# Long convolution in the frequency domain: the filters' spectrum K in one copy, four frequencies on each half of the partitions

## The chip, the core and the metric

The kernel runs on one core of a Trainium2 chip. Its engines work side by side, each through a queue of its own in order: PE multiplies matrices (PEld are its weight loads), DVE (VectorE) and POOL (GpSimd) work elementwise, ACT (ScalarE) copies, casts and applies functions, and SP (SyncE) issues the DMAs. The metric is the device time of one execution in microseconds (us).

## The reference

One block of a diffusion backbone of two layers: attention, then a Hyena layer. The change touches only the second, on 1024 tokens x 1024 channels:

```python
def long_conv(u, k_f, skip):
    L = u.shape[1]
    uf = _f32(u)
    y = jnp.fft.irfft(jnp.fft.rfft(uf, n=2 * L, axis=1) * k_f, n=2 * L, axis=1)[:, :L]
    return (y + uf * _f32(skip)).astype(u.dtype)

def hyena_mixer(h, w_in, conv_w, conv_b, ..., freq, skip, w_out):
    p = h @ w_in                                    # four times the width
    u = short_conv(p[..., :(HY_ORDER + 1) * HY_WIDTH], conv_w, conv_b)
    gate = p[..., (HY_ORDER + 1) * HY_WIDTH:]
    parts = jnp.split(u, HY_ORDER + 1, axis=-1)
    k_f = hyena_filters(L, ...)
    z = parts[0]
    for o in range(HY_ORDER):                       # HY_ORDER = 2
        z = parts[o + 1] * long_conv(z, k_f[:, o], skip[o])
    return (z * jax.nn.silu(gate)) @ w_out
```

So for each of two orders and each channel a signal is transformed, multiplied by the filter's spectrum k_f, with the skip weight added to it, and transformed back.

## The kernel before, in words

The filters' spectra are made early, next to the attention, and lie in DRAM as `Kd`. After the attention comes the stage that the change touches, the function `projections`: 32 jobs (four kinds times eight blocks of 128 channels) multiply the normed tokens by `hy_w_in`, each product as three matmuls on high and low parts (`mm3`, L100 to L102), into a PSUM tile `pw`. The weights are split into `wh` (ACT, L1711) and `wl` (POOL, L1712) a job ahead. The stage is cut into pieces of two `mm3`; after each piece the functions run that a table `plan` holds for its number, put there by `at(piece, function)`. That fixes by hand the order of the instructions on PE, ACT, DVE and POOL. The order of SP's DMAs is not written by hand: it is laid down when the program is built, by when each is expected to be ready. Each engine keeps to its order, so one that waits holds up all behind it.

Sixteen convolutions (two orders, eight blocks) run between the projections, one begun every 13 pieces (`start`, `PERIOD`). `conv(o, b)` places its steps s_ pieces after its start:

- 0 to 3, `first`: one stage of the transform on PE, a copy by ACT (L1827, tile `caT`), a store to DRAM (`ad`, L1828).
- 4, `regroup`: `ad` is read back in another order as two tiles `cau` (L1833).
- 11, 13, 15, 17, `spectrum(0)` to `spectrum(3)`: each takes four of sixteen frequency groups through eight matmul passes (L1854) into a PSUM bank `ps` from `pq`, with real parts on partitions 0 to 63 and imaginary ones on 64 to 127. Then DVE multiplies by K: two products across the halves into `cB` (L1857, L1858), one in place into `cA` (L1860), and their sum (L1861).
- 4 pieces behind each, `back`: matmuls (L1871), a copy by ACT into `cbT` (L1873), a store `bd` (L1876).
- 22 and later: `regroup_back` loads `spare` (L1881), `split_back` splits it (ACT `cih` L1887, DVE `cil` L1888), `last` does the last matmuls on `IA`, `end` multiplies into the gated product `u` (L1913).

`pq()` hands out PSUM banks in turn, so a matmul may wait for the engine that still reads its bank. Between these steps DVE does the short convolutions (L1781 to L1784), POOL the low halves `z1l` (L1905) and the gates (L1773).

K comes by `kernel_load(uc)`, four times in a convolution, two of them at piece 4, the others at pieces 12 and 14. Each fills a tile of 128 partitions with two DMAs (L1842) of the same 64 rows, one to each half, since `spectrum` reads K at the partitions of its PSUM operand. For the first there is also the skip row `skp` (L1839), a DMA that overwrites row 64 of the tile, where a real coefficient of its own lies (L1844), and two memsets (L1845, L1846). POOL adds the skip weights (L1847). Two buffers serve K, so a load waits until the `spectrum` two before it has been read by DVE.

Of the kernel before, what the change touches and what calls it, by code (L numbers as in the profile page):

```python
# [9 lines left out]
F32 = mybir.dt.float32  # L10
# [98 lines left out]
def backbone(tc, I, out):  # L109
# [1704 lines left out]
    def conv(o, b):  # L1814
# [20 lines left out]
        def kernel_load(uc):  # L1835
            us = slice(4 * uc, 4 * uc + 4)
            if uc == 0:
                B["skp"] = yp.tile([P, P], F32, tag="skp", bufs=2, name=nm("skp"))
                nc.sync.dma_start(B["skp"], I["hy_skip"][0, o, b * P:(b + 1) * P].partition_broadcast(P))  # L1839
            K = yp.tile([P, 2, 4, P], F32, tag="K", bufs=2, name=nm("K"))  # L1840
            for h in range(2):
                nc.sync.dma_start(K[64 * h:64 * h + 64], Kv[:, :, us, :])  # L1842
            if uc == 0:
                nc.sync.dma_start(K[64:65, 0, 0, :], Kd[o, b, 64:65, 0:P])  # L1844
                nc.gpsimd.memset(K[0:1, 1, 0, :], 0.0)  # L1845
                nc.gpsimd.memset(K[64:65, 1, 0, :], 0.0)  # L1846
            nc.gpsimd.tensor_tensor(K[:, 0], K[:, 0], B["skp"].unsqueeze(1).to_broadcast([P, 4, P]), ALU.add)  # L1847
            Ks[uc] = K

        def spectrum(uc):  # L1850
            K, au = Ks.pop(uc), B["au", uc // 2]
            ps = pq()
            for i in range(4):
                nc.tensor.matmul(ps[:, i * P:(i + 1) * P], FB[:, 4 * uc + i, :], au[:, 4 * (uc % 2) + i, :], start=True, stop=True)  # L1854
            pv = ps.rearrange("p (u c) -> p u c", c=P)
            B_ = yp.tile([P, 4, P], F32, tag="cB", bufs=2, name=nm("cB"))
            nc.vector.scalar_tensor_tensor(B_[0:64], pv[64:128], -1.0, K[64:128, 1], ALU.mult, ALU.mult)  # L1857
            nc.vector.tensor_tensor(B_[64:128], pv[0:64], K[0:64, 1], ALU.mult)  # L1858
            A1 = yp.tile([P, 4, P], F32, tag="cA", bufs=2, name=nm("cA"))
            nc.vector.tensor_tensor(A1, pv, K[:, 0], ALU.mult)  # L1860
            nc.vector.tensor_tensor(A1, A1, B_, ALU.add)  # L1861
            A1s[uc] = A1
# [59 lines left out]
        at(s_ + 4, lambda: kernel_load(0), regroup, lambda: kernel_load(1))  # L1922
        for i in range(4):
            at(s_ + SP + 2 * i, lambda i=i: spectrum(i))
            if i < 2:
                at(s_ + SP + 2 * i + 1, lambda i=i: kernel_load(i + 2))
# [367 lines left out]
```

## Time and profile before

| | |
|---|---|
| time, median of three runs | 1821.87 us (1821.21 to 1828.35) |
| profiled execution, its own time | 1821.09 us |
| its span | 1819.3 us |
| busy share of the span: PE, DVE, POOL, ACT | 95%, 57%, 48%, 43% |
| DMA over the span | 253.28 MB, mean 139 GB/s |

The span runs from the first to the last instruction; the profiled execution's own time contains it and what lies around. A wait is given as engine and line that waited, then what ended it, the total in us, how often, and the longest. In a row of a timeline the number first is the start in us from the span's beginning, then the duration. In grouped rows the busy time is followed by the mean ns of one instruction, and behind the second bar stands the idle time of the engine just before them and what ended it.

### The profile page before, as it was taken

What the parts mean: (1) busy time and instruction counts of PE and PEld (TensorE: products, weight loads), DVE (VectorE), ACT (ScalarE), POOL (GpSimd) and SP (SyncE); (2) the same over time, 40 slices, a digit from 0 to 9 for tenths busy, and PEclk for the clock granted to TensorE, in tenths of its full rate; (3) what the DMA queues carried; (4) which work ended last, traced back from release to release, by engine and by line L of the source; (5) the groups of instructions that cost most, each with busy time, mean ns of one, the idle gap of its engine ahead of it and who ended that gap; (6) DMA issues with size and microseconds to landing.
All of it is one profiled execution on the core that took longest, in us unless ns stands there. A gap on an engine that the chain in (4) does not pass through costs nothing.

```text
span 1819.3 us, 25906 instructions
## 1 busy us (share of the span) xinstructions
PE 1725.1 (95%) x9616; PEld 1346.1 (74%) x9616; DVE 1029.7 (57%) x1495; ACT 774.3 (43%) x1326; POOL 865.6 (48%) x615
## 2 busy tenths in 40 slices
PE   7999999998999999899999999999999999899898
PEld 2667789986766666666666788888888788788686
DVE  5557757446666665466565323456657555645743
ACT  5878711243545544544444333243343333332431
POOL 2457712534379777577776453234333333244400
PEclk9999999999999999999999999999999999999999
DMA  7766688232120010100010227568787778787633
GB/s 256 246 211 216 210 257 276 64 82 74 43 56 24 11 47 21 39 32 22 22 34 21 81 88 184 161 178 221 215 228 223 223 217 219 209 239 212 196 98 110
DMA packets 245709, 253.28 MB, mean 139 GB/s; under 512 B 30591, under 2 KB 195367, under 8 KB 245167
## 3 DMA queue, kind: packets, MB, share of 16 engines
q1 hardware_dynamic: 243408, 249.53, 46.4%
q10 hardware_dynamic: 2176, 2.10, 0.4%
q8 instruction: 76, 1.25, 0.3%
q14 instruction: 49, 0.40, 0.1%
HBM read 169.65 MB, written 61.94 MB: 127 GB/s over the span
## 4 chain that ended last, share of the span: by engine, by line
PE 57%; DVE 7%; DMA 5%; POOL 3%; issue 2%; ACT 2%; SPq 1%; DVEq 0%; POOLq 0%; ACTq 0%
PE pw L1277 8%; PE pw L102 8%; PE pw L100 8%; PE pw L101 8%; PE pv L1180 7%; DMA K<-Kd 4%; PE pq L989 3%; PE pq L100 2%; PE pq L101 2%; PE pq L102 2%; PE pq L1871 2%; PE pq L1854 2%; DVE mx L990 2%; PE pq L1212 1%; POOL wl L1712 1%
## 5 line engine op out<-in xcount | busy, mean ns | idle before, releaser
L1294 ACT ACTIVATE PT<-pw 128x1024 f32<-128x1024 f32 x160 | 163.7, 1025 | 171.8 <-PE pw L1277 160.4
L990 DVE TENSOR_REDUCE mx<-pq 128x1 f32<-128x512 f32 x256 | 170.9, 683 | 112.9 <-PE pq L989 111.1
L100 PE MATMUL pw<-h1h,wh 128*128 128x512 f32 x512 | 209.4, 409 | 0.0
L102 PE MATMUL pw<-h1h,wl 128*128 128x512 f32 x512 | 202.7, 396 | 4.4 <-POOL wl L1712 4.4
L101 PE MATMUL pw<-h1l,wh 128*128 128x512 f32 x512 | 201.2, 393 | 0.0
L1847 POOL TENSOR_TENSOR K<-K,skp 128x512 f32<-128x512 f32 x64 | 86.3, 1350 | 217.8 <-DMA K<-Kd 196.1
L1189 POOL TENSOR_TENSOR acc<-acc,PT 128x1024 f32<-128x1024 f32 x62 | 147.5, 2379 | 22.3 <-ACT PT L1294 20.7
L102 PEld LDWEIGHTS pw<-h1h,wl 128*128 128x128 f32 x512 | 96.8, 189 | 26.8 <-POOL wl L1712 5.3
L101 PEld LDWEIGHTS pw<-h1l,wh 128*128 128x128 f32 x512 | 97.0, 189 | 17.8
L546 POOL TENSOR_TENSOR kacc<-kacc,kabs 128x512 f32<-128x512 f32 x56 | 72.4, 1294 | 79.1 <-ACT kabs L544 77.2
L100 PEld LDWEIGHTS pw<-h1h,wh 128*128 128x128 f32 x512 | 97.0, 189 | 17.5
L1712 POOL TENSOR_TENSOR wl<-wr,wh 128x1024 fp32r<-128x1024 f32 x32 | 79.5, 2483 | 54.9 <-ACT wh L1711 54.9
L1857 DVE SCALAR_TENSOR_TENSOR cB<-pq,K 64x512 f32<-64x512 f32 x64 | 44.4, 693 | 107.0 <-DMA K<-Kd 38.5
L1827 ACT COPY caT<-pq 128x512 f32<-128x512 f32 x64 | 37.6, 588 | 146.0 <-PE pq L102 104.0
L1187 POOL TENSOR_TENSOR acc<-PT,PT 128x1024 f32<-128x1024 f32 x31 | 73.9, 2385 | 53.7 <-ACT PT L1294 50.4
L572 PE MATMUL pq<-au,FBk 128*128 128x256 f32 x256 | 68.6, 391 | 11.6 <-DVE kc L583 10.1
L1888 DVE TENSOR_TENSOR cil<-spare,cih 128x512 fp32r<-128x512 f32 x64 | 54.4, 888 | 44.3 <-ACT cih L1887 44.3
L1873 ACT COPY cbT<-pq 128x512 f32<-128x512 f32 x64 | 37.5, 587 | 95.4 <-PE pq L1871 49.7
L1180 PE MATMUL pv<-PT,Va 128*64 128x256 f32 x640 | 77.9, 385 | 0.0
L1180 PE MATMUL pv<-PT,Vm 128*64 128x256 f32 x640 | 77.7, 385 | 0.0
L1854 PE MATMUL pq<-cau,FB 128*128 128x128 f32 x512 | 69.7, 280 | 8.1 <-DVE cA L1860 7.0
L1871 PEld LDWEIGHTS pq<-cA,GB 128*128 128x128 f32 x512 | 68.3, 195 | 11.8 <-issue 6.5
(449 smaller groups left out, 4705.8 us busy)
## 6 DMA issues: line engine op xcount, KB each, us to landing
K<-Kd SPq DMA_DIRECT2D x128, 256.0 KB
au<-aT SPq DMA_DIRECT2D x128, 128.0 KB
space<-in_ada_w_dram SPq DMA_DIRECT2D x32, 512.0 KB
wr<-in_hy_w_in_dram SPq DMA_DIRECT2D x32, 512.0 KB
ad<-caT SPq DMA_DIRECT2D x64, 256.0 KB
cau<-ad SPq DMA_DIRECT2D x32, 512.0 KB
bd<-cbT SPq DMA_DIRECT2D x32, 512.0 KB
spare<-bd SPq DMA_DIRECT2D x64, 256.0 KB
```

What stands on the lines that cost most here:

```text
L100: nc.tensor.matmul(ps, lh, rh, start=start, stop=False)
L101: nc.tensor.matmul(ps, lh, rl, start=False, stop=False)
L102: nc.tensor.matmul(ps, ll, rh, start=False, stop=stop)
L990: nc.vector.reduce_max(m[:, i, j:j + 1], ps, axis=AX.X)
L1180: nc.tensor.matmul(ps[64 * e:64 * e + 64, 0:256], vals[:, 2 * s + j], PT[:, j, 256 * e:256 * e + 256], start=s == 0 and j == 0, stop=s == ...
L1189: eng.tensor_tensor(accs[gi], accs[gi], PT, ALU.add)
L1277: nc.tensor.matmul(ps[:, 512 * j:512 * j + 512], l[:, kt * P:(kt + 1) * P], r, start=i == 0, stop=i == len(passes) - 1)
L1294: nc.scalar.activation(PT, ps.rearrange("p (a q) -> p a q", q=512), AF.Exp, scale=SC_A if kind == 0 else SC_M)
L1712: nc.gpsimd.tensor_tensor(wl, f(r), f(wh), ALU.subtract)
L1847: nc.gpsimd.tensor_tensor(K[:, 0], K[:, 0], B["skp"].unsqueeze(1).to_broadcast([P, 4, P]), ALU.add)
L1854: nc.tensor.matmul(ps[:, i * P:(i + 1) * P], FB[:, 4 * uc + i, :], au[:, 4 * (uc % 2) + i, :], start=True, stop=True)
L1871: nc.tensor.matmul(ps[:, i * P:(i + 1) * P], GB[:, 4 * uc + i, :], A1[:, i, :], start=True, stop=True)
```

## The change

`kernel_load(h)` now loads half a convolution's K: its tile holds eight frequency groups, four on partitions 0 to 63 and the next four on 64 to 127, each by one DMA. There are two such loads in a convolution, at pieces 4 and 5, which fill both buffers. `spectrum(uc)` reads the half of the tile that holds its four groups, whatever the partitions of its PSUM operand. The one product of 128 partitions into `cA` becomes two of 64. The coefficient that had been patched into row 64 gets a tile of its own, `k0`, with the skip added by POOL, and one more DVE product of one row in the first `spectrum`.

```diff
--- before.py
+++ after.py
@@ -1832,32 +1832,34 @@
                 au = B["au", h] = yp.tile([P, 8, P], F32, tag="cau", bufs=2, name=nm("cau"))
                 nc.sync.dma_start(au, ad.rearrange("g (j u) c -> (g j) u c", u=16)[:, 8 * h:8 * h + 8])
 
-        def kernel_load(uc):
-            us = slice(4 * uc, 4 * uc + 4)
-            if uc == 0:
+        def kernel_load(h):
+
+            K = Ks[h] = yp.tile([P, 2, 4, P], F32, tag="K", bufs=2, name=nm("K"))
+            for e in range(2):
+                nc.sync.dma_start(K[64 * e:64 * e + 64], Kv[:, :, 8 * h + 4 * e:8 * h + 4 * e + 4, :])
+            if h == 0:
                 B["skp"] = yp.tile([P, P], F32, tag="skp", bufs=2, name=nm("skp"))
                 nc.sync.dma_start(B["skp"], I["hy_skip"][0, o, b * P:(b + 1) * P].partition_broadcast(P))
-            K = yp.tile([P, 2, 4, P], F32, tag="K", bufs=2, name=nm("K"))
-            for h in range(2):
-                nc.sync.dma_start(K[64 * h:64 * h + 64], Kv[:, :, us, :])
-            if uc == 0:
-                nc.sync.dma_start(K[64:65, 0, 0, :], Kd[o, b, 64:65, 0:P])
+                k0 = B["k0"] = yp.tile([P, P], F32, tag="k0", bufs=1, name=nm("k0"))[64:65]
+                nc.sync.dma_start(k0, Kd[o, b, 64:65, 0:P])
                 nc.gpsimd.memset(K[0:1, 1, 0, :], 0.0)
-                nc.gpsimd.memset(K[64:65, 1, 0, :], 0.0)
+                nc.gpsimd.tensor_tensor(k0, k0, B["skp"][64:65], ALU.add)
             nc.gpsimd.tensor_tensor(K[:, 0], K[:, 0], B["skp"].unsqueeze(1).to_broadcast([P, 4, P]), ALU.add)
-            Ks[uc] = K
 
         def spectrum(uc):
-            K, au = Ks.pop(uc), B["au", uc // 2]
+            K, au = Ks[uc // 2][64 * (uc % 2):64 * (uc % 2) + 64], B["au", uc // 2]
             ps = pq()
             for i in range(4):
                 nc.tensor.matmul(ps[:, i * P:(i + 1) * P], FB[:, 4 * uc + i, :], au[:, 4 * (uc % 2) + i, :], start=True, stop=True)
             pv = ps.rearrange("p (u c) -> p u c", c=P)
             B_ = yp.tile([P, 4, P], F32, tag="cB", bufs=2, name=nm("cB"))
-            nc.vector.scalar_tensor_tensor(B_[0:64], pv[64:128], -1.0, K[64:128, 1], ALU.mult, ALU.mult)
-            nc.vector.tensor_tensor(B_[64:128], pv[0:64], K[0:64, 1], ALU.mult)
+            nc.vector.scalar_tensor_tensor(B_[0:64], pv[64:128], -1.0, K[:, 1], ALU.mult, ALU.mult)
+            nc.vector.tensor_tensor(B_[64:128], pv[0:64], K[:, 1], ALU.mult)
             A1 = yp.tile([P, 4, P], F32, tag="cA", bufs=2, name=nm("cA"))
-            nc.vector.tensor_tensor(A1, pv, K[:, 0], ALU.mult)
+            for e in range(2):
+                nc.vector.tensor_tensor(A1[64 * e:64 * e + 64], pv[64 * e:64 * e + 64], K[:, 0], ALU.mult)
+            if uc == 0:
+                nc.vector.tensor_tensor(A1[64:65, 0, :], pv[64:65, 0, :], B["k0"], ALU.mult)
             nc.vector.tensor_tensor(A1, A1, B_, ALU.add)
             A1s[uc] = A1
 
@@ -1919,11 +1921,10 @@
         s_ = start[o, b]
         for i in range(4):
             at(s_ + i, lambda i=i: first(i // 2, i % 2))
-        at(s_ + 4, lambda: kernel_load(0), regroup, lambda: kernel_load(1))
+        at(s_ + 4, lambda: kernel_load(0), regroup)
+        at(s_ + 5, lambda: kernel_load(1))
         for i in range(4):
             at(s_ + SP + 2 * i, lambda i=i: spectrum(i))
-            if i < 2:
-                at(s_ + SP + 2 * i + 1, lambda i=i: kernel_load(i + 2))
             at(s_ + SP + 2 * i + GBD, lambda i=i: back(i))
         at(s_ + IB, lambda: regroup_back(0))
         at(s_ + IAP - SA, lambda: split_back(0))
```

How the rows stand in the built program, at three places. DVE, the first spectrum of the first convolution, before:

```order
L1857 SCALAR_TENSOR_TENSOR cB_10456<-pq_10451,K_10369 64x512
L1858 TENSOR_TENSOR cB_10456<-pq_10451,K_10369 64x512
L1860 TENSOR_TENSOR cA_10459<-pq_10451,K_10369 128x512
L1861 TENSOR_TENSOR cA_10459<-cA_10459,cB_10456 128x512
L1857 SCALAR_TENSOR_TENSOR cB_10483<-pq_10478,K_10380 64x512
```

and now:

```order
L1856 SCALAR_TENSOR_TENSOR cB_10457<-pq_10452,K_10367 64x512
L1857 TENSOR_TENSOR cB_10457<-pq_10452,K_10367 64x512
L1860 TENSOR_TENSOR cA_10460<-pq_10452,K_10367 64x512 x2
L1862 TENSOR_TENSOR cA_10460<-pq_10452,k_2059_10372 1x128
L1863 TENSOR_TENSOR cA_10460<-cA_10460,cB_10457 128x512
L1856 SCALAR_TENSOR_TENSOR cB_10482<-pq_10477,K_10367 64x512
```

The second spectrum reads the same K tile as the first, and the product into cA stands twice, with the one-row product behind it once in a convolution.

SP's queue between two convolutions in the middle of the stage, around the stores `ad` of one of them, before (K_11379 belongs to the convolution before it):

```order
L1842 DMA K_11379<-Kd 64x2x512 x2
L1828 DMA ad_9368<-caT_11383 128x4x128
L1828 DMA ad_9368<-caT_11414 128x4x128
L1842 DMA K_11470<-Kd 64x2x512
L1828 DMA ad_9368<-caT_11435 128x4x128
L1881 DMA spare_10076<-bd_9365 128x4x128 x2
L1876 DMA bd_9367<-cbT_11396 128x1024
L1842 DMA K_11470<-Kd 64x2x512
L1833 DMA cau_11477<-ad_9368 128x1024
L1833 DMA cau_11479<-ad_9368 128x1024
L1844 DMA K_11470<-Kd 1x128
L1842 DMA K_11481<-Kd 64x2x512 x2
```

and now:

```order
L1844 DMA k_2234_11465<-Kd 1x128
L1828 DMA ad_9368<-caT_11360 128x4x128
L1828 DMA ad_9368<-caT_11373 128x4x128
L1839 DMA K_11460<-Kd 64x2x512 x2
L1828 DMA ad_9368<-caT_11405 128x4x128
L1828 DMA ad_9368<-caT_11426 128x4x128
L1883 DMA spare_10076<-bd_9365 128x4x128 x2
L1878 DMA bd_9367<-cbT_11386 128x1024
L1833 DMA cau_11470<-ad_9368 128x1024
L1833 DMA cau_11472<-ad_9368 128x1024
L1839 DMA K_11492<-Kd 64x2x512 x2
```

K_11379, the last quarter of the convolution before, no longer stands among the stores; the one-row load stands ahead of them, and of this convolution's K there is one load among the stores and one behind the `cau` loads.

POOL at the same place, before:

```order
L1847 TENSOR_TENSOR K_11345<-K_11345,skp_11198 128x512
L1847 TENSOR_TENSOR K_11379<-K_11379,skp_11198 128x512
L1845 MEMSET K_11470 1x128
L1846 MEMSET K_11470 1x128
L1847 TENSOR_TENSOR K_11470<-K_11470,skp_11468 128x512
L1847 TENSOR_TENSOR K_11481<-K_11481,skp_11468 128x512
L1712 TENSOR_TENSOR wl_10021<-wr_10008,wh_10010 128x1024
```

and now:

```order
L1845 MEMSET K_11460 1x128
L1846 TENSOR_TENSOR k_2234_11465<-k_2234_11465,skp_11463 1x128
L1847 TENSOR_TENSOR K_11460<-K_11460,skp_11463 128x512
L1712 TENSOR_TENSOR wl_10021<-wr_10008,wh_10010 128x1024
L1847 TENSOR_TENSOR K_11492<-K_11492,skp_11463 128x512
L1712 TENSOR_TENSOR wl_10022<-wr_10009,wh_10011 128x1024
```

Two adds on K stand in a convolution where four stood, and the weight splits wl stand between or behind them.

## The prediction

> **What bounds the kernel now.** I read the page's first part, then the busy times of the stage that the change touches (from 1120 us, just ahead of the first load of K, to 1745 us, after the last convolution), then the waits inside it, and last the chain and the timelines around the longest waits.
>
> ```profile
> span 1819.3 us, 25906 instructions
> PE 1725.1 (95%) x9616; PEld 1346.1 (74%) x9616; DVE 1029.7 (57%) x1495; ACT 774.3 (43%) x1326; POOL 865.6 (48%) x615
> 1120.00:1745.00 625.00, 594.96 (x3150) 503.99 (x3149) 367.82 (x481) 217.98 (x331) 222.75 (x154) 0.98 0.74 210
> ```
>
> The third row gives the stage's length and the busy times of PE, PEld, DVE, ACT and POOL, then the granted clock, the share of the DMA engines and GB/s. PE is busy for 595.0 of 625 us, and the change neither adds nor removes a matmul. So all that can be won are PE's 30.0 us of waits and what a lowered clock costs. Here is what ended those waits (total us, times, longest):
>
> ```profile
> PE pq L1854 <- DVE cA L1860: 7.0, 3, 3.5
> PE pq L1871 <- DVE cA L1861: 5.5, 1, 5.5
> PE pw L102 <- POOL wl L1712: 4.4, 2, 3.4
> PE pq L101 <- DVE cil L1888: 4.4, 4, 1.9
> PE pq L100 <- DVE u L1913: 2.8, 2, 2.1
> PE pq L100 <- ACT cih L1887: 2.6, 1, 2.6
> PE pq L1791 <- DVE u L1783: 1.2, 1, 1.2
> PE pq L1854 <- issue: 1.1, 1, 1.1
> PE pq L101 <- POOL z1l L1905: 1.0, 2, 0.7
> ```
>
> They sum to 30.0 us. No DMA is named, but DVE and POOL work in order, so I asked what had held them. The chain around the longest of the L1854 waits, and DVE's timeline ahead of three others:
>
> ```profile
> 1538.99 6.47 DMA K<-Kd
> 1545.56 0.69 DVE cB L1857
> 1550.22 0.43 PE pw L100
> 1553.29 0.23 PE pw L100
> ...
> 1242.45 0.69 DVE L1857 SCALAR_TENSOR_TENSOR cB<-pq,K 64x512 f32<-64x512 f32 x1 [5.69 <-DMA K<-Kd]
> ...
> 1618.78 0.69 DVE L1857 SCALAR_TENSOR_TENSOR cB<-pq,K 64x512 f32<-64x512 f32 x1 [7.50 <-DMA K<-Kd]
> ...
> 1653.13 0.69 DVE L1857 SCALAR_TENSOR_TENSOR cB<-pq,K 64x512 f32<-64x512 f32 x1 [2.91 <-DMA K<-Kd]
> ```
>
> A quarter's K lands 6.5 us after its issue, DVE stands still until then, and PE's next spectrum finds its PSUM bank still unread. I put all three L1854 waits (7.0 us) and two of the four cil waits (those after 1242 and 1653 us, about 3.9 us) on late K: **10.9 us by way of DVE**. POOL holds PE in the same manner:
>
> ```profile
> 1567.72 1.28 POOL L1847 TENSOR_TENSOR K<-K,skp 128x512 f32<-128x512 f32 x1 [2.43 <-PE pw L101]
> 1568.96 2.79 POOL L1712 TENSOR_TENSOR wl<-wr,wh 128x1024 fp32r<-128x1024 f32 x1
> ...
> 1429.99 1.30 POOL L1847 TENSOR_TENSOR K<-K,skp 128x512 f32<-128x512 f32 x1 [3.18 <-DVE cB L1858]
> ```
>
> The weight split wl stands behind an add on K, and PE then waits 3.4 us for wl. The rows name another engine as the one that let the add go; I read it as the load, since POOL's adds wait for K 196 us in all (the L1847 row below). Both wl waits (4.4), both z1l waits (1.0) and the longer L1913 wait (2.1, behind the add at 1430 us) are of this kind: **7.5 us by way of POOL**. The other 11.6 us are plain backlog of DVE, or ACT's cih.
>
> The clock adds a cost. In the chain above the matmuls after the stall come every 0.43 us, later every 0.23, and the granted clock says why:
>
> ```profile
> 1548.90:1552.30 3.40, 3.40 (x10) 2.66 (x9) 3.31 (x5) 1.83 (x3) 1.27 (x1) 0.50 0.88 242
> 1572.80:1576.20 3.40, 3.40 (x15) 3.23 (x14) 1.21 (x2) 0.00 (x0) 0.00 (x0) 0.50 0.92 247
> 1658.10:1661.50 3.40, 3.40 (x12) 2.86 (x12) 2.73 (x5) 0.00 (x0) 1.28 (x1) 0.50 1.07 264
> ```
>
> With the one at 1620.6 us there are four such stretches, each right behind a wait that I put on K; at half clock for 3.4 us each costs 3.4 / 2 = 1.7 us, 6.8 us together. A fifth, of 6.8 us, follows the 5.5 us wait at the stage's end.
>
> **The change part by part.** *Fewer, earlier loads.* 64 of the 128 quarter-megabyte loads go: 64 x 0.262 MB = 16.8 MB of the 131 MB that 210 GB/s moves in 625 us, 13% of the traffic, and 64 issues from SP:
>
> ```profile
> L1842 SPq DMA_DIRECT2D K<-Kd x128: 573/583/1576, 1124.3 to 1707.0; - x128
> SPq L1844 <- DMA K<-Kd: 62.9, 14, 7.1
> SPq L1842 <- DVE cA L1860: 40.6, 25, 10.7
> DVE cB L1857 <- DMA K<-Kd: 38.5, 9, 9.9
> DVE cB L1857 <- DMA skp<-in_hy_skip_dram: 9.5, 1, 9.5
> 1463.81 0.89 PE pq L1854 x8
> 1495.63 0.89 PE pq L1854 x8
> ```
>
> 64 x 0.58 = 37 us of SP's time go, and with them the second row: the patch of row 64 (L1844) wrote into K and had to let K land first, holding the au loads behind it in the queue. Now it has a tile of its own. From the last two rows a convolution's 13 pieces take 31.8 us, 2.45 us a piece. Before, the third quarter's load was issued one piece after the first spectrum and used three pieces later, 7.3 us, against 6.5 of flight and the wait for the buffer. Now the second buffer's load is freed by the last spectrum of the convolution before (piece 4 of this one) and used at piece 15: 11 pieces, 27 us. Taking off some 5 us for DVE's reads, two issues, 7 of flight and 1.3 of POOL's add leaves 12 us in hand; the first buffer has as much. So DVE's waits on K and the skip row (38.5 + 9.5 = 48.0 us) go, and I book the 10.9 us fully.
>
> *POOL.* 32 of 64 adds and 16 memsets go, and 16 adds on one row come:
>
> ```profile
> L1847 POOL TENSOR_TENSOR K<-K,skp 128x512 f32<-128x512 f32 x64 | 86.3, 1350 | 217.8 <-DMA K<-Kd 196.1 <-PE pq L102 8.5 <-DMA ad<-caT 3.9
> L1858 DVE TENSOR_TENSOR cB<-pq,K 64x512 f32<-64x512 f32 x64 | 43.8, 685 | 1.9
> L1860 DVE TENSOR_TENSOR cA<-pq,K 128x512 f32<-128x512 f32 x64 | 44.3, 692 | 2.0
> L1861 DVE TENSOR_TENSOR cA<-cA,cB 128x512 f32<-128x512 f32 x64 | 63.4, 991 | 2.2
> L1782 DVE SCALAR_TENSOR_TENSOR u<-pw,cw,u x24: 331/340/344, 1123.0 to 1679.4; 128x127 f32<-128x127 f32 x24
> ```
>
> 32 x 1.35 = 43 us of POOL's time. POOL still waits, though: the add on the second buffer now follows one piece behind the first, and its load still waits for DVE, so wl behind it can be late again. Of the 7.5 us I take two thirds, 5.0 (bounds 0 and 7.5).
>
> *The price, on DVE.* K now lies on one half of the partitions, so the multiply of L1860 becomes two. The rows say that width is free and count is not: 64 partitions take 685 ns, 128 take 692. With the 0.03 us that lies between these operations (1618.78, next one 0.72 later by the mean plus that gap) the 64 extra ones cost 64 x 0.72 = 46 us. The 16 one-row multiplies have their nearest row in L1782, 0.34 us for 127 columns: 16 x 0.37 = 6 us. Together 52 us, DVE's busy share rising from 59% to 67%. Behind each stand the add of L1861, the bank that PE wants back, cil, y and u. Cover: DVE's own idle time, which contains the 48 us of waits that vanish. A gain stands against it: L1861 takes 991 ns on the mean, L1860 692 on equally many elements; L1861 reads two SBUF tiles, and the long ones lie beside POOL's work. Half the adds on K gone takes a fifth of POOL's 222.75 us, hence about a fifth of those 64 x 0.30 = 19 us: 3.8.
> What stays on PE's path is where DVE was late without K: the 5.5 us at the end (three spectra in a row before it, +2.2), the issue wait (two, with one row, +1.8), the two other cil waits (+1.4), the short u wait (+0.7) and L1783 (+0.7): 6.8. Some 3 us are added for places that had less than 0.7 us in hand, 3.8 taken off for the shorter L1861: **+6.0 us**. Lower bound 2 (the end alone); upper bound 52, if no extra operation had cover.
>
> *The clock.* Three of the four stretches follow waits booked fully (5.1 us), the fourth a wait of POOL's at two thirds (1.1): 6.2 us; bounds 0 and 6.8.
>
> The Trainium skill speaks to this in "TensorE: Matmul & The Clock Gate", section "What's actually happening": the clock falls after at least one idle window of about 3.4 us, in windows that run freely. By that rule only the waits of 3.5 and 3.4 us would carry a stretch, 3 us in all for the sum instead of 6, and the time would be about 1808. The trace goes further than the rule: the half clock also followed the 1.9 us wait near 1655 us.
>
> **Sum.** The profiled execution took 1821.1 us (span 1819.3, 1.8 around it), 0.8 under the median of 1821.87. 1821.1 - 10.9 - 5.0 - 6.2 + 6.0 = 1805.0; I say **1805**, 0.9% faster.
>
> **The rivals.**
> *DVE takes K's place (slower).* If the extra operations meet no idle time, as in the burst of spectrum, short convolution and cil, each delays PE by 0.72 us. The 22.1 us booked (10.9 + 5.0 + 6.2) are gone once 31 of the 64 do, and the time is slower than before from there: 45 of them give 1821 - 22 + 32 = 1831, all, with the one-row ones, 1821 - 22 + 52 = 1851. For it: 22.0 of the 30.0 us name DVE or its issue. Against: four of PE's waits on cil in 62 matmul pairs, and 48 us of blockage that goes. Chance 0.11.
> *The next late thing (no change).* The second buffer hangs on DVE still, so POOL waits as long in one piece as before in three; wl, z1l and u stay late (7.5 us not won, 1.7 of clock), and half of the DVE part is taken by au and spare, which then land last: 1821 - 5.5 - 2.5 + 6.0 = 1819, with fewer new stalls 1814. For it: cih has waited on a transfer already (2.6 us). Against: 13% less traffic and SP's 63 us wait gone. Chance 0.20.
> *All of it is won.* The POOL part in full, cih too, and the DVE price at its lower bound: 1821.1 - 10.9 - 7.5 - 2.6 - 6.8 + 2 = 1795. For it: the order of POOL puts wl behind only two adds on K per convolution. Chance 0.13.
> *It doesn't prefetch.* The load could be issued no earlier than the old one if SP sits on the wait for DVE; then the bytes alone are saved. In the issue order the second buffer's load stands behind both au loads, far ahead of its use; I count it in with no change.
>
> **How the numbers follow.** My forecast (1799 to 1812) has 0.56, all won 0.13, no change 0.20, slower 0.11. The range for 8 in 10 runs from 1793 to 1822: the lower end is all won with 2 us more from the shorter L1861, the upper one no change plus a little. 0.5% is 9.1 us, about what a measurement of this kernel can tell. Faster (under 1812.8) gets 0.56 + 0.13 = 0.69, same 0.20, slower 0.11.
>
> **What would show it.** Right: the waits of DVE's first spectrum operation on K near zero; POOL's waits on K down from 196 us but not gone; no half-clock stretch between 1540 and 1665 us; DVE busier by about 50 us in the stage; L1861's mean below 950 ns; PE's waits in the stage near 15 us, most of them naming DVE. Wrong: DVE still waiting for K, or PE's waits on cil and cA above 20 us, which is the first rival, or waits on wl as before, which is the second. The forecast fails if DVE's backlog, not K, set the L1854 waits.

## The result

Measured together on one chip, the kernel before took 1825.11 us (median of 4 runs, 1821.21 to 1830.2) and the changed kernel 1808.41 us (4 runs, 1803.32 to 1815.76). The ratio is 0.992, with a 95% interval of 0.9893 to 0.9947: faster by 0.8%. A second comparison on another chip, told below, gave 0.9907 (0.9888 to 0.9926), 0.9% faster. The forecast was 1821.1 to 1805.0 us, a ratio of 0.991.

The profiled execution of the changed kernel has a span of 1813.9 us. Its part ahead of the first spectrum took 6.8 us longer than in the profile shown of before (37 us of it were at half clock, against 24), so what the change did is read from the stage: from the first matmul of a spectrum to the last matmul of a back transform. These are the rows of the two groups, with the starts of the first and of the last matmul; of the changed kernel:

```profile
L1853 PE MATMUL pq<-cau,FB x512: 270/275/422, 1156.6 to 1706.5; 128*128 128x128 f32 x171
L1873 PE MATMUL pq<-cA,GB x512: 270/275/550, 1163.9 to 1720.9; 128*128 128x128 f32 x171
```

and of the kernel before:

```profile
L1854 PE MATMUL pq<-cau,FB x512: 270/275/553, 1149.8 to 1712.0; 128*128 128x128 f32 x171
L1871 PE MATMUL pq<-cA,GB x512: 270/275/553, 1157.1 to 1725.8; 128*128 128x128 f32 x171
```

From 1156.6 to 1720.9 and from 1149.8 to 1725.8, with the last matmul's own 0.4 us: the stage went from 576.4 to 564.7 us, 11.7 us shorter. "The stage" below is this length, taken in the same way for every kernel from its one profiled execution; a second profile of the changed kernel gave 564.4.

### The profile page after: what moved, and what is told of

Read it like the earlier page. It is cut to its first block, busy times and chain, and to the rows that moved or that the text cites. A ratio compares the mean times of both kernels' runs of the same rounds, so it can differ in the third digit from the quotient of the medians.

```text
span 1813.9 us, 25833 instructions
## 1 busy us (share of the span) xinstructions
PE 1727.4 (95%) x9616; PEld 1349.0 (74%) x9616; DVE 1075.8 (59%) x1575; ACT 775.1 (43%) x1326; POOL 819.9 (45%) x583
## 5 line engine op out<-in xcount | busy, mean ns | idle before, releaser
L1189 POOL TENSOR_TENSOR acc<-acc,PT 128x1024 f32<-128x1024 f32 x62 | 147.4, 2377 | 22.3 <-ACT PT L1294 20.7
L1847 POOL TENSOR_TENSOR K<-K,skp 128x512 f32<-128x512 f32 x32 | 42.5, 1330 | 122.4 <-DMA K<-Kd 119.9
L1860 DVE TENSOR_TENSOR cA<-pq,K 64x512 f32<-64x512 f32 x128 | 88.1, 688 | 1.8
L572 PE MATMUL pq<-au,FBk 128*128 128x256 f32 x256 | 68.1, 390 | 12.1 <-DVE kc L583 10.6
L1875 ACT COPY cbT<-pq 128x512 f32<-128x512 f32 x64 | 37.5, 587 | 97.3 <-PE pq L1873 68.1
L1873 PE MATMUL pq<-cA,GB 128*128 128x128 f32 x512 | 68.8, 278 | 7.6 <-DVE cA L1863 6.6
```

What stands on the lines that cost most here:

```text
L1189: eng.tensor_tensor(accs[gi], accs[gi], PT, ALU.add)
L1860: nc.vector.tensor_tensor(A1[64 * e:64 * e + 64], pv[64 * e:64 * e + 64], K[:, 0], ALU.mult)
L1873: nc.tensor.matmul(ps[:, i * P:(i + 1) * P], GB[:, 4 * uc + i, :], A1[:, i, :], start=True, stop=True)
```

## The profile after

The busy times of the changed kernel in the window that the prediction used (PE, PEld, DVE, ACT, POOL; granted clock, DMA share, GB/s):

```profile
1120.00:1745.00 625.00, 604.56 (x3204) 511.43 (x3202) 417.76 (x569) 220.55 (x333) 175.48 (x122) 0.99 0.64 186
```

DVE works 417.8 us instead of 367.8, 50 us more, as the prediction's 52 us had it; POOL 175.5 instead of 222.8; the DMA share is 0.64 instead of 0.74. PE's waits in the stage:

```profile
PE pq L1873 <- DVE cA L1863: 6.6, 3, 5.2
PE pq L101 <- DVE cil L1890: 4.3, 4, 3.0
PE pq L1853 <- issue: 3.7, 2, 1.8
PE pq L100 <- DVE u L1915: 2.9, 2, 2.1
PE pq L1791 <- DVE cA L1860: 1.4, 2, 0.9
PE pq L1873 <- DVE cA L1860: 1.1, 3, 0.6
PE pq L1791 <- DVE u L1783: 0.2, 1, 0.2
```

They sum to 20.2 us, against 30.0. The three spectra that waited for a PSUM bank held by L1860 (7.0 us) are gone, and so are the waits on wl and z1l (5.4 us). What is left names DVE, or is the issue wait. No wait of DVE's products names a load of K any more; one, of 3.8 us, names POOL's add on K. POOL's waits still name K's loads, though less (196.1 us before, for the adds):

```profile
POOL wl L1712 <- ACT wh L1711: 127.5, 16, 18.0
POOL K L1847 <- DMA K<-Kd: 119.9, 21, 13.5
```

The first row is a change of role: POOL now arrives ahead of its weight splits and waits for ACT 127.5 us (52.8 before). The groups on which the price and the relief were worked out:

```profile
L1860 DVE TENSOR_TENSOR cA<-pq,K 64x512 f32<-64x512 f32 x128 | 88.1, 688 | 1.8
L1863 DVE TENSOR_TENSOR cA<-cA,cB 128x512 f32<-128x512 f32 x64 | 59.0, 922 | 2.2
L1847 POOL TENSOR_TENSOR K<-K,skp 128x512 f32<-128x512 f32 x32 | 42.5, 1330 | 122.4 <-DMA K<-Kd 119.9 <-PE pq L1873 1.9
```

The product over 64 partitions takes 688 ns, where one over 128 took 692, and the add into cA 922 instead of 991.

The clock: the part from 1540 to 1665 us, where four half-clock stretches had stood in the row of stalls before, is clean, but there are new ones elsewhere.

```profile
1217.80:1221.20 3.40, 3.40 (x16) 3.00 (x14) 2.14 (x4) 0.50 (x1) 0.00 (x0) 0.50 0.55 139
1501.10:1507.90 6.80, 6.05 (x18) 5.18 (x19) 3.01 (x5) 0.59 (x1) 0.15 (x1) 0.50 0.60 166
1540.00:1665.00 125.00, 121.51 (x670) 103.52 (x669) 88.89 (x123) 43.22 (x68) 36.55 (x26) 1.00 0.70 199
```

In the last of these windows the kernel before had PE busy for 113.2 us at a clock of 0.95. The stretch at 1501 us follows the 3.0 us wait on cil. The timelines of POOL and DVE ahead of it show what remained:

```profile
1497.67 1.29 POOL L1847 TENSOR_TENSOR K<-K,skp 128x512 f32<-128x512 f32 x1 [13.12 <-DMA K<-Kd]
1498.91 2.34 POOL L1712 TENSOR_TENSOR wl<-wr,wh 128x1024 fp32r<-128x1024 f32 x1
...
1499.35 3.05 DVE L1890 TENSOR_TENSOR cil<-spare,cih 128x512 fp32r<-128x512 f32 x2
```

POOL stood 13 us on a load of K, then did the add, then wl; and beside wl two cil operations took 3.05 us. In DVE's timeline of the kernel before, two of them while POOL stood idle:

```profile
1183.77 1.29 DVE L1888 TENSOR_TENSOR cil<-spare,cih 128x512 fp32r<-128x512 f32 x2 [7.33 <-ACT cih L1887]
```

This order (load, add, the work queued behind it, a DVE operation stretched beside that work) comes back in the experiments.

## The experiments

The first theory was the prediction's: late K is the loss, by way of DVE and of POOL, and the split of the product is a price of some 6 us. The rivals were that the price is larger, that the saved bytes carry the gain, and that the number of POOL's adds does. Every experiment was timed in five rounds beside the kernel before, on one of three chips; its ratio is against the kernel before on the same chip.

| kernel | time (us) | ratio, 95% interval | stage (us) |
|---|---|---|---|
| the change (first, again) | 1808.4, 1808.5 | 0.992 (0.9893 to 0.9947), 0.9907 (0.9888 to 0.9926) | 564.7, 564.4 |
| the change, one product | 1796.9 | 0.9849 (0.9826 to 0.9871) | 549.2 |
| before, split product only | 1839.5 | 1.0084 (1.0059 to 1.0110) | 594.1 |
| one copy, late quarters | 1824.5 | 0.9998 (0.9981 to 1.0015) | 580.2 |
| the change, copies that moved ahead of the stage | 1819.1 | 0.9967 (0.9951 to 0.9984) | 562.1 |
| the change, 64 adds on POOL | 1810.4 | 0.9924 (0.9905 to 0.9943) | 565.3 |
| the change, traffic given back in the stage | 1808.8 | 0.9913 (0.9893 to 0.9932) | 559.5 |
| only the real part on both halves | 1790.9 | 0.9826 (0.9801 to 0.9850) | 544.8 |
| adds into cA on POOL | 1791.2 | 0.9812 (0.9791 to 0.9834) | 546.5 |
| before, no adds on K | 1801.3 | 0.9864 (0.9846 to 0.9881) | 552.3 |
| one copy, late quarters, no adds | 1803.9 | 0.9875 (0.9857 to 0.9893) | 558.8 |
| the change, no adds | 1809.2 | 0.9891 (0.9871 to 0.9911) | 559.8 |

### The price of the split

The change with the product into cA put back into one instruction (its factors then belong in part to another quarter):

```diff
-            for e in range(2):
-                nc.vector.tensor_tensor(A1[64 * e:64 * e + 64], pv[64 * e:64 * e + 64], K[:, 0], ALU.mult)
+            nc.vector.tensor_tensor(A1, pv, Ks[uc // 2][:, 0], ALU.mult)
```

> The changed kernel, but the product into cA is again one instruction of 128 partitions, which reads K at the partitions of its PSUM operand; so half of it takes the wrong four frequencies, and the output is not the reference's. It takes the price of the split away and keeps all else. Theory (early K wins some 16 to 22 us, the split costs about 6): 6 us faster than the change, ratio to before 0.988 to 0.990; PE's waits in the stage fall from 20 to 13 us or less, and DVE's busy time in the stage falls by 44 us. Rival (the split costs PE 15 us or more, since most of the waits left name DVE): 0.983 or less, waits under 8 us. Rival (the split is free, all 46 us beside other work): 0.992, waits near 20 us.

Measured: 1796.88 us; the ratio, 0.9849, lies between the theory's 0.988 and the 0.983 of the rival with the larger price. PE's waits in the stage fall from 20.2 to 10.9 us:

```profile
PE pq L1872 <- DVE cA L1862: 5.4, 2, 4.5
PE pq L1853 <- issue: 2.3, 2, 1.1
PE pq L100 <- DVE u L1914: 1.9, 2, 1.7
PE pq L101 <- DVE cil L1889: 1.3, 3, 0.6
```

And the kernel before with nothing but the split:

```diff
-            nc.vector.tensor_tensor(A1, pv, K[:, 0], ALU.mult)
+            for e in range(2):
+                r = slice(64 * e, 64 * e + 64)
+                nc.vector.tensor_tensor(A1[r], pv[r], K[r, 0], ALU.mult)
```

> The kernel before, with K loaded as before, twice and late, and only the product into cA split in two. It adds the price alone. Theory: 6 us slower than before, 1.002 to 1.005, since K's waits stay and the extra 46 us of DVE sit behind them; PE's waits in the stage 34 to 40 us. Rival (DVE's extra work takes every slack): 1.015 or more, waits over 50 us. Rival (free): 1.000.

Measured: 1839.47 us, 0.84% slower than before, again between what the theory and its rival said. PE's waits are 44.1 us in all; three of the larger ones, with DVE's wait on K:

```profile
PE pq L1854 <- DVE cA L1862: 10.2, 4, 4.1
PE pq L101 <- DVE cil L1890: 7.7, 4, 3.1
PE pq L101 <- POOL z1l L1907: 5.9, 5, 2.5
...
DVE cB L1857 <- DMA K<-Kd: 34.2, 9, 9.8
```

The two agree. The split costs 564.7 - 549.2 = 15.5 us of the stage in the one, 594.1 - 576.4 = 17.7 in the other; in time, by the ratios, 0.992 or 0.9907 less 0.9849 is 11 to 13 us, and 0.0084 is 15. The one-row product is in the first kernel still, so these are the 64 extra operations alone. The term was 6.0. Their own length was booked right; what was too small is how much of it reaches PE. The profiles divide the price in two. PE's waits are 9.3 us more with the split in the one pair (20.2 against 10.9) and 14.1 in the other (44.1 against 30.0). The rest is clock: a stretch of the stage at half clock costs half its length, and that makes 7.7 us against 1.6 in the one pair, 12.0 against 8.5 in the other. Together they give 15.4 and 17.6 us, nearly the whole of the two differences. Without the split the change would have won 27 us.

### Early filling, bytes, and the number of adds

One copy of K and the split product, but in quarters that are loaded at the old pieces, each with an add of 64 partitions (the edit is shown against the change, and only in part):

```diff
-        at(s_ + 4, lambda: kernel_load(0), regroup)
-        at(s_ + 5, lambda: kernel_load(1))
+        at(s_ + 4, lambda: kernel_load(0), regroup, lambda: kernel_load(1))
...
+            if i < 2:
+                at(s_ + SP + 2 * i + 1, lambda i=i: kernel_load(i + 2))
```

> One copy of K and the split as in the change, the tile of its own for the patched row, but K in quarters at the pieces of before (4, 4, 12, 14), each into the lower half of a tile. So the bytes are halved and K is as late as before. Theory (early filling carries the gain): 0.998 to 1.003, DVE waiting for K 20 us or more in the stage, wl and z1l again among PE's waits. Rival (half the bytes carry it, since each load lands sooner): 0.992 to 0.994, DVE's waits on K under 8 us.

Measured: 1824.52 us, no gain. Its rows contradict the theory that DVE's stand on K is what costs:

```profile
DVE cB L1858 <- DMA K<-Kd: 4.9, 2, 3.8
...
L1848 POOL TENSOR_TENSOR K<-K,skp 64x512 f32<-64x512 f32 x64 | 86.3, 1351 | 249.4 <-DMA K<-Kd 202.5 <-DVE cA L1862 14.5 <-PE pq L1875 14.3
L1865 DVE TENSOR_TENSOR cA<-cA,cB 128x512 f32<-128x512 f32 x64 | 71.8, 1123 | 2.2
```

With half the bytes K is there when DVE wants it (4.9 us of waits, 38.5 before), yet PE waits 34.3 us in the stage (wl and z1l, which the theory expected there, are not among these waits). POOL waits for K as long as before, 202.5 us, and the add into cA has become longer, 1123 ns.

Against the rival of the bytes, copies that nothing reads were added to the change, behind the loads of K:

```diff
+            for e in range(2):
+                scr = dram.tile([64, 2, 4, P], F32, tag="scr", bufs=4, name=nm("scr"))
+                nc.sync.dma_start(scr, Kv[:, :, 8 * h + 4 * e:8 * h + 4 * e + 4, :])
```

> The changed kernel with 64 loads more of the same 256 KB, issued right behind K's, from Kd to a scratch in DRAM that nobody reads: the traffic and SP's issues of before are back, the early filling stays. Theory: 0.992 to 0.995, DVE's waits on K near zero. Rival (the bytes carry the gain): 0.998 or more, with K, cau or spare landing late in DVE's or ACT's waits.

Measured: 1819.13 us, ratio 0.9967 (0.9951 to 0.9984). This run decides nothing. The copies hung on nothing in the stage and were moved ahead of it; the stage has a DMA share of 0.65, where the change has 0.64, and takes 562.1 us, 2.6 less than in the change. The time was lost ahead of the stage, which begins at 1165.0 us instead of 1156.6. So the copies were tied to the stage, as reads of the store `ad` of the same convolution:

```diff
+        def traffic():
+            for i in range(4):
+                scr2 = dram.tile([4, P, P], F32, tag="dummy", bufs=4, name=nm("dummy"))
+                nc.sync.dma_start(scr2, ad[4 * i:4 * i + 4])
...
-        at(s_ + 5, lambda: kernel_load(1))
+        at(s_ + 5, lambda: kernel_load(1), traffic)
```

> The change, with the 1 MB of K loads that it saves in a convolution given back as four 256 KB copies from one DRAM buffer to another, of the stored ad of the same convolution, issued behind the second load of K; nothing reads the copies. The theory that the bytes are no part of the gain once K is asked for early: the DMA share of the stage up from 0.64 to 0.74 or more, the time within 3 us of the change, DVE's waits on K still under 5 us. The rival that the saved traffic is itself what brings K, au and spare in time: waits of DVE on K or of PE on au and spare come back, at least 5 us on PE, time 1814 or more.

Measured: 1808.81 us, the time of the change. The window from 1115 to 1740 us shows the traffic there:

```profile
1115.00:1740.00 625.00, 606.94 (x3230) 513.94 (x3229) 421.90 (x570) 222.21 (x335) 184.44 (x122) 0.99 0.71 213
```

213 GB/s, above the 210 of the kernel before, at a DMA share of 0.71 (0.74 before), and the gain stays. So the saved traffic is no measurable part of it.

The number of adds: the change with each add on K cut into two of 64 partitions.

```diff
-            nc.gpsimd.tensor_tensor(K[:, 0], K[:, 0], B["skp"].unsqueeze(1).to_broadcast([P, 4, P]), ALU.add)
+            for e in range(2):
+                r = slice(64 * e, 64 * e + 64)
+                nc.gpsimd.tensor_tensor(K[r, 0], K[r, 0], B["skp"][r].unsqueeze(1).to_broadcast([64, 4, P]), ALU.add)
```

> The change, with each of POOL's adds on K cut into two adds of 64 partitions each, so that 64 of them stand in the stage as before; loads, buffers and the split product stay as the change has them. The theory that the halved number of POOL adds carries a good part of the gain (they stretch DVE's L1863 add beside them, and hold wl): POOL busy in the stage about 40 us more than the change's 175, the mean of the add into cA up from 922 to about 1010 ns, so 64 x 0.09 = 6 us more of DVE, PE's waits up from 20 to about 28 us, time 7 to 12 us above the change (1815 to 1821). The rival that early filling alone carries it, whatever POOL adds: the mean under 950 ns, PE's waits within 3 us of 20, time within 3 us of the change.

Measured: 1810.43 us, 2 us from the change and not to be told from it; POOL is busy 49 us longer (224.3 us in the window). The add into cA takes 981 ns, between the 1010 of the theory and the 950 of its rival. The theory expected 7 to 12 us of time and falls: the number of the adds is no measurable part of the gain either. Between the late quarters and this kernel the number and the size of the adds are the same; what differs is when K is asked for, and with it when the adds are done.

### POOL's adds taken away

That led to three kernels without the adds on K: before, the late quarters and the change. They leave the skip weights out of the spectrum. The edit is one line in each (and the one-row add, where there is one):

```diff
-            nc.gpsimd.tensor_tensor(K[:, 0], K[:, 0], B["skp"].unsqueeze(1).to_broadcast([P, 4, P]), ALU.add)
```

> The kernel with one copy of K loaded in quarters at the old pieces and with the split product, without POOL's adds on K (the skip row is left out of the spectrum, so the result lacks the skip term). The theory that early filling gained because it moved POOL's adds: asked for late they wait for K (202.5 us on POOL), hold wl, u and z1l behind them, and lie beside DVE's add into cA (mean 1123 ns). Without them the mean falls under 960 ns, PE's waits from 34 to 20 us or less, the time from 1824.5 to 1805 to 1812, that of the change. The rival that the late loads themselves cost (DVE's operations and the transfers of au and spare around them): the time stays above 1816.

> The change without POOL's adds on K (the skip row is left out of the spectrum, so the result lacks the skip term). The theory that early filling has already taken POOL's adds out of the way: at most 5 us under the change, 1803 to 1809, PE's waits 16 to 20 us. The rival that the adds still cost much (POOL waits 120 us for K in the change too, and wl, z1l stand behind): more than 8 us under the change, below 1800.

> The kernel before, without POOL's adds on K (the skip row is left out of the spectrum, so the result lacks the skip term). K still lands late, so DVE still stands on K (38.5 us before); POOL no longer does, but for the memsets. The theory that POOL's adds, being late, made most of the loss in the kernel before: 10 to 18 us under it, 1808 to 1816, with the waits on wl and z1l (5.4 us) gone and the add into cA under 900 ns. The rival that late K costs by way of DVE, as the prediction booked it (10.9 us that way and 7.5 by way of POOL): 5 to 9 us under it, 1817 to 1821, the waits of DVE on K near 38 us and PE's L1854 waits near 7 us.

> The change itself once more, beside the three kernels without adds, on the chip on which they run: 1804 to 1813 and a ratio to before of 0.989 to 0.995 if the first comparison holds.

Measured: the late quarters 1803.85 us, the change without adds 1809.21, before without adds 1801.34, the change itself 1808.53. So the adds cost 20.7 us in the late quarters (1824.52 less 1803.85, on two chips; 22 by the ratios), 24 us in the kernel before (1825.35 on the same chip), and nothing that could be measured in the time of the change, though its stage is 4.9 us shorter without them. The gain in the kernel before is larger than either theory had it. Its rows, of PE's waits, DVE's wait on K and the waits in SP's queue:

```profile
PE pq L1870 <- DVE cA L1860: 7.0, 4, 4.5
PE pq L100 <- ACT cih L1886: 3.0, 1, 3.0
PE pq L1853 <- issue: 2.1, 2, 1.0
PE pq L101 <- DVE cil L1887: 1.0, 2, 0.7
...
DVE cB L1856 <- DMA K<-Kd: 11.8, 4, 4.7
...
SPq L1706 <- POOL wl L1712: 34.2, 16, 6.6
SPq L1810 <- POOL u L1773: 12.8, 3, 7.3
```

Every load of K is asked for at its old piece, in the old two copies and all the old bytes; and yet DVE's waits on K fall from 38.5 to 11.8 us, the three L1854 waits on a bank are gone, and PE waits 13.1 us instead of 30.0. SP's order is nearly the old one: 116 of the 144 DMAs into K have the same weight loads, stores and reads ahead of them, most of the others one weight load more or less. One thing moved with the adds, though: the 16 loads of the skip row, which nothing reads now, all go out before 1170 us, so the 9.5 us that DVE had waited for one of them are gone too. No run tells what part of the 24 us that is.

So it was not the place of the loads alone that made K late. The missing link is in SP's queue. In the kernel before:

```profile
SPq L1706 <- POOL wl L1712: 78.0, 18, 7.5
SPq L1810 <- POOL u L1773: 23.2, 3, 10.3
```

and around the stall at 1545 us that the prediction had shown, first POOL, then SP with its wait between 1529 and 1541 us, then DVE:

```profile
1529.69 1.30 POOL L1847 TENSOR_TENSOR K<-K,skp 128x512 f32<-128x512 f32 x1 [6.79 <-DMA K<-Kd]
1530.94 1.30 POOL L1905 TENSOR_TENSOR z1l<-y,z1h 128x512 fp32r<-128x512 f32 x1
1532.21 2.85 POOL L1712 TENSOR_TENSOR wl<-wr,wh 128x1024 fp32r<-128x1024 f32 x1
1535.02 2.89 POOL L1773 TENSOR_TENSOR u<-u,sg 128x1024 f32<-128x1024 f32 x1
...
1530.93 0.93 SPq L1881 DMA_DIRECT2D spare<-bd  x2
1537.94 0.33 SPq L1810 DMA_DIRECT2D zd<-u  x1
1538.36 1.24 SPq L1842 DMA_DIRECT2D K<-Kd  x2
...
SPq L1810 <- POOL u L1773: 6.0, 1, 6.0
...
1545.56 0.69 DVE L1857 SCALAR_TENSOR_TENSOR cB<-pq,K 64x512 f32<-64x512 f32 x1 [9.87 <-DMA K<-Kd]
```

It is a loop. POOL stands 6.8 us on one load of K; behind its add, in order, come z1l, wl and u; SP stands 6.0 us on that u (the store zd), with the next load of K right behind it in the queue; that load is issued at 1538.4, lands at 1545.5, and DVE has stood 9.9 us on it. The add at the head of POOL's queue turns one late load into the next. The same order stands ahead of all four of DVE's waits that the prediction had shown: after an add that waited 4.1, 6.8, 3.6 and 3.3 us for K, SP stood 5.2 us on wl before 1233 us, 6.0 on u before 1538, 10.3 on u before 1611 and 7.5 on wl before 1643, and each time K's load came right behind, or behind one pair of `spare` loads.

Taking the adds away breaks the loop. The change escapes it in another way: POOL still waits 119.9 us for K and SP 59.8 on wl, but K is asked for so long before its use that a late issue no longer reaches DVE. So the totals of these waits are no measure by themselves: without adds POOL's two memsets on the first quarter still stand idle, 200 us against 101 before, and in the late quarters without adds SP waits 75.0 us on wl while no wait of DVE names K.

The adds have a second way to cost. In the late quarters DVE hardly waited for K (4.9 us), so K that comes late to DVE can't be their 20 us; there the add into cA falls from 1123 to 932 ns without POOL's adds, 12 us of DVE's time. At the stage's end one case is plain: POOL stands 6.9 us on K, adds from 1716.2 us and has another operation (L1982) behind it; beside these two, two DVE operations (L1948) take 4.67 us and PE then waits 8.5. Without the adds POOL is idle there, the same two take 1.29 us, and PE waits 5.1. In the kernel before, too, the add into cA falls without them, from 991 to 765 ns, 14 us. But the change with one product has 981 ns and wins 27 us, so in that layout the longer add alone costs little; how the 24 us of the kernel before divide between the two ways stays open.

Without adds the split is cheap, too: late quarters against before, 558.8 - 552.3 = 6.5 us of the stage, and 0.0011 of the time, which the intervals don't tell from nothing. (These two differ also in the bytes, which the run above found to be worth nothing.) The change without adds, which has the split and early K, stands 12 us above the change with one product by the two times, some 8 by their ratios (0.9891 less 0.9849), 10.6 by the stage, though it has no adds at all; so with early K the split keeps a price of 8 us or more, adds or not. Why it is smaller where K is late and the adds are gone stays open.

### Two versions that keep the gain and not the price

First, the real part of K alone on both halves, in quarters and three buffers, the imaginary part once in two buffers. The product is one instruction of 128 partitions again, the patched row lies in the tile, cB has one buffer instead of two, and the adds stand two pieces or more ahead of their use (only a part of the edit is shown):

```diff
+            nc.vector.tensor_tensor(A1, pv, Ks[uc], ALU.mult)
...
+        at(s_ + 4, lambda: real_load(0), lambda: imag_load(0), lambda: real_load(1), regroup)
+        at(s_ + 5, lambda: imag_load(1), lambda: real_load(2))
+        at(s_ + 12, lambda: real_load(3))
+        for i in range(4):
+            at(s_ + (7, 9, 11, 15)[i], lambda i=i: kernel_add(i))
```

> A third layout: the real part of K lies on both halves of the partitions as before the change (three buffers of a quarter each, the add on a quarter two pieces ahead of its use), the imaginary part once, as in the change (two buffers). The product into cA is one instruction of 128 partitions again and the patched row lies in the tile, so the 64 + 16 extra DVE operations are gone; three quarters of the old bytes of K, 64 POOL adds. The theory that the change's gain is early filling and its price the split: DVE busy in the stage about 382 us as in the run with one product, time 1797 to 1803, under the change. The rival that the halved POOL adds carry much of it: the add into cA near 1000 ns, POOL about 220 us, PE's waits above 20 us, time 1805 to 1812.

Measured: 1790.93 us, 1.7% faster than before, more than forecast, and the stage at 544.8 us; PE waits 7.5 us in it, 4.5 of that once, at its end:

```profile
PE pq L1880 <- DVE cA L1870: 5.3, 2, 4.5
...
L1857 POOL TENSOR_TENSOR Kr<-Kr,skp 128x512 f32<-128x512 f32 x64 | 84.3, 1323 | 54.4 <-DMA Kr<-Kd 49.4 <-DMA Ki<-Kd 5.1
```

It has 64 adds on POOL, as the kernel before has, and three quarters of its bytes of K. POOL's adds wait 54 us for K there, not 196, and its memsets, which stood idle 101 us before, not at all.

Second, the change with its adds on K later and the add of cB into cA given to POOL:

```diff
-            nc.vector.tensor_tensor(A1, A1, B_, ALU.add)
+            nc.gpsimd.tensor_tensor(A1, A1, B_, ALU.add)
...
+        at(s_ + 8, lambda: kernel_add(0))
+        at(s_ + 12, lambda: kernel_add(1))
```

> The change, with POOL's two adds on K moved later (behind the weight splits, two to three pieces ahead of their use) and the add of cB into cA (L1863) moved from DVE to POOL. DVE loses 64 x 0.92 = 59 us in the stage, which more than pays the split; POOL gains 64 x about 1.35 us, from its add on K of the same size, = 86 us. The theory that what bounds the change now is DVE's backlog: PE's waits that name DVE fall below 10 us, time 1795 to 1803. The rival that POOL becomes the late engine, since cA now takes 0.4 us more each and stands behind adds on K and weight splits: PE waits on POOL's cA or wl, 15 us or more, time 1808 to 1820.

Measured: 1791.2 us, the same. DVE is busy 41 us less between 1115 and 1740 us (378.4 against 419.7), which nearly pays for the split's 44; POOL's adds on K wait 1.3 us in all, since they are taken up only when K is there. POOL's own add into cA takes 1394 ns, and PE waits for POOL once, 6.7 us at the stage's end, where DVE had held it for 5.2. Both versions beat the change by about 1%; against the change with one product their medians are lower, but the intervals overlap.

## Why the prediction was right, point by point

The time was forecast at 1805, 0.88% under its base, and measured 0.80% and 0.93% under it. That it came so close is partly luck: the gains were booked some 5 us too low and the price 5 to 9 us too low, and the two errors cancel.

- **The 10.9 us by way of DVE: won, for a cause that was only half named.** The waits of DVE's products on K's loads went, and with them the L1854 waits. (The two cil waits booked with 3.9 us are 1.92 and 1.84, 3.8 in all.) The step that failed is "a quarter's K lands 6.5 us after its issue, DVE stands still until then", read as a matter of the load's place: in the kernel before without adds the loads are asked for at the same place, and the L1854 waits vanish. The issue was late because SP stood on POOL's u and wl, and these stood behind POOL's add on K. The prediction counted what an add holds on PE directly (wl, z1l, u) and did not follow what it holds through SP.
- **The 5.0 of 7.5 us by way of POOL: about right in direct effect, and too small as a cause.** wl and z1l (5.4 us) went, the u waits did not (2.8 before, 2.9 after). But taking POOL's adds away, with the split and the layout left alone, gave 24 us in the kernel before, nearly as much as the gross gain of 27.
- **The gains together: 22.1 us booked, about 27 won.** The change with one product is 1.5% under before, 27.6 us by the ratio, and its stage 27.2 us shorter. This is the rival "all of it is won" in its gains.
- **The price of the split, +6.0 us: too small by a factor of about two.** Its DVE time was right (50 us against 52). On PE's path it was 15.5 us of the stage, 11 to 15 of the time. By the prediction's own 0.72 us an operation, that is 15 to 21 of the 64 operations meeting a late DVE, where the sum had found some eight. The waits listed as places where DVE was late without K were too few, because late DVE moves: a burst that had 0.7 us in hand becomes a stall with the next wl or cil beside it. "Some 3 us are added for places that had less than 0.7 us in hand" is the step that should have been larger. A second term is missing from the price: the new waits bring half clock, 6.1 us of the 15.5. The slower rival, DVE takes K's place, was right in kind: in the kernel before the split alone is slower by 0.84%.
- **The clock, -6.2 us: not won in the profile.** The four stretches between 1540 and 1665 us went as foretold, but new waits of DVE's backlog brought others (1217.8, and 6.8 us at 1501.1), and the stage lost 7.7 us to half clock where it had lost 8.5. In the version with one product it lost 1.6: the clock's gain was there without the split, and the split took it back.
- **SP's wait on the patch.** The 62.9 us of L1844 did not simply go. In the change the one-row load waits 33.5 us for DVE's one-row product, and the skip row's load 37.5 us for POOL's add. No run shows a cost of it.
- **The next late thing.** It was there, but smaller than that rival had it: POOL still waits 119.9 us for K, and the 3.0 us wait at 1498 us comes from it. Moving the adds later, with the add into cA on POOL, brought their wait to 1.3 us.
- **What would show it.** As foretold: no wait of DVE's spectrum operations on a load of K, POOL's waits down but not gone, the clean clock from 1540 to 1665 us, DVE busier by 50 us, L1863 at 922 ns (under 950). Not as foretold: PE's waits, 20.2 us instead of some 15; 9.3 of them go with the split.

## What to carry to other kernels

An operation that waits for a load costs by what is queued behind it on its own engine, and by whose issue waits for that: follow the queue round once more, to the next load, before a stall is put on the load. A cheap test is to leave the waiting operation out; here that gave 24 us, more than the whole change. And an extra operation on an engine that is busy two thirds of the time was not hidden here by the other third: of 64 extra operations of 0.7 us, about a quarter to a third came out on the path.

## What the runs showed of the hardware

*DVE's adds beside POOL's work.* In the kernel before, 34 of the 64 adds into cA had no operation of POOL beside them: they took 693 ns on the mean. The others took up to 2.75 us. One case of the kernel before, POOL first:

```profile
1202.01 2.38 POOL L1712 TENSOR_TENSOR wl<-wr,wh 128x1024 fp32r<-128x1024 f32 x1
...
1201.68 0.69 DVE L1860 TENSOR_TENSOR cA<-pq,K 128x512 f32<-128x512 f32 x1
1202.41 2.53 DVE L1861 TENSOR_TENSOR cA<-cA,cB 128x512 f32<-128x512 f32 x1
```

wl ends at 1204.39; the add, begun at 1202.41, ends at 1204.94, 0.55 us behind it: nearly its whole length after POOL's operation. The product L1860, which reads PSUM and one SBUF tile, took 0.69 us with wl beside its second half, and 692 ns on the mean of all 64. The Trainium skill states this in "SBUF — State Buffer", section "Who interferes with whom": a DVE operation with two inputs in SBUF contends with a GpSimd operation that reads SBUF, one with a single SBUF input does not, outside DVE's two-port modes. The trace agrees with both halves. It bears on the case in that the time of POOL's work counted for more than its amount. With 64 adds on K of the same size the mean of the add into cA was 1123 ns when K was late and 981 when it was early; with 32 early adds it was 922 and 889 in the two profiles of the change, and the time was the same as with 64.

*The half clock.* In the changed kernel two waits of 1.8 us (the issue waits of L1853 ahead of 1217 and 1477 us) went different ways: the stretch at 1217.8 us followed the first, while behind the second the clock stayed at 1.00:

```profile
1477.90:1481.30 3.40, 3.40 (x21) 3.00 (x22) 2.82 (x5) 1.55 (x4) 0.00 (x0) 1.00 0.58 133
```

So a wait under 2 us may or may not cost 1.7 us more. The Trainium skill, "TensorE: Matmul & The Clock Gate", section "What's actually happening", speaks of windows that run freely and of an idle window of about 3.4 us; free windows would fit that equal waits differ, but a wait of 1.8 us is short of an idle window, and the trace has half clock behind it all the same.
